# Moving the shared expert slots ahead of the last 14 own slots, and spacing the gathers by 0.88 of TensorE's work, in a two-layer diffusion backbone

## The chip, the core and the metric

The kernel runs on one core of a Trainium2 chip, as one program. The metric is the time of one execution in microseconds on the device; times are the median of several runs. The engines of a core are TensorE (PE in the rows; PEld loads its weights), VectorE (DVE), ScalarE (ACT), GpSimd (POOL) and SyncE (SP). Each works through its own queue of instructions in the order in which the program holds them, and they wait for each other through semaphores. DMA moves data between device memory (HBM) and the on-chip buffers. DMA transfers are issued by SP, ScalarE and GpSimd.

## The reference

256 latent tokens of width 1024 pass through two layers. Layer 0 mixes them with a state-space scan and latent attention, layer 1 with a chunked gMLP; each layer then applies a PEER expert network, which this change is about:

```python
def _peer(h, wq, k1, k2, u_tab, v_tab):          # 128 x 128 experts, 8 heads, 16 experts a head
    q = (t @ wq).reshape(n_tok, PEER_HEADS, PEER_DKEY)
    s1 = jnp.einsum('thd,hkd->thk', q[..., :half], k1)
    s2 = jnp.einsum('thd,hkd->thk', q[..., half:], k2)
    v1, i1 = lax.top_k(s1, PEER_TOPK)
    v2, i2 = lax.top_k(s2, PEER_TOPK)
    ...
    top_s, j = lax.top_k(cand_s, PEER_TOPK)      # of the 256 sums of a head
    gate = jax.nn.softmax(top_s.astype(jnp.float32), axis=-1)
    ...
        act = gelu(einsum('phkd,pd->phk', take(u_tab, ib), tb))
        return einsum('phk,phkd->pd', gb * act, take(v_tab, ib))
```

A token so adds up 128 experts: for each, the dot of its row of `u` with the token, a gelu, the gate, and the row of `v` with that weight. Then `x = x + g2 * peer(...)`. Everything is float32.

## The kernel before

`peer(l)` runs once in each layer. The experts fall into 128 classes by their first key. The first X = 70 classes are done densely, for all tokens: `products()` streams their weights (512 KB loads `wr<-in_dn` into four buffers) and issues to TensorE first 70 score units (`pa<-phf,wr`) and then 70 units of second products (`pb<-wr,ge`), which add up in four PSUM banks `py`. In the order rows a unit is 8 matmuls; the trace shows 16 records of it. Between the two lies the spread: 32 blocks turn each token's chosen keys into weights for the dense classes. A block is `o`, `eq` and `oc` on VectorE, 16 matmuls `pb<-oc,o` on TensorE, and a `ge` row with ScalarE and VectorE. All blocks must be done before the first unit of second products.

The experts in the other classes are gathered for each token, by `gather()`. A slot is one expert for each of the 128 tokens of a tile. There are CAP = 62 own slots for each of two tiles, 124. For each, GpSimd issues an indirect DMA of 128 x 2048 floats, 1.05 MB (`rows<-in_uv,gidx`), VectorE takes the dot with the tokens (`junk<-rows,h`), ScalarE makes the weight `wt`, and LAG = 2 slots later VectorE accumulates (`acc<-rows,wt,acc`). Tokens with more experts put the rest into a list, from which SHARED = 2 shared slots are filled. A shared slot takes two of the NR = 7 row buffers: the expert's row, and the token's row (`rows<-hs,lidx`, 128 x 1024, 0.52 MB). After its dot VectorE makes the matrix `sc` (`sc<-iotaL,spot,wt`), and TensorE multiplies it with the expert's row and adds to `py` (`pb<-rows,sc`, 8 matmuls in the order rows, 16 records in the trace). So 126 slots and 126 dots a layer. `take()` picks the next 24 keys of a tile on VectorE, `listing()` makes the shared list.

When all is added up, `ending()` multiplies and adds `acc`, `overflow()` reads from `fi` whether there are more experts than fit (a branch, not taken here), and `x` is updated from `py`, `acc` and the rest (`x<-pb,ge`).

The order of instructions on each engine is fixed when the program is built. `schedule()` asks the streams `products()`, `gather()`, `choose()` and `ending()` in turn, by a clock kept for each engine (`clk["T"]` for TensorE, `clk["V"]` for VectorE), which is an estimate; at run time each engine waits for what it needs, whatever the clocks said. Three rules of `gather()` matter. After each slot it waits until `clk["T"]` passes `nxt[0]`, which grows by PACE times the rest of TensorE's time for each remaining slot. It also holds while `urgent()` says that spread blocks are pressing. And a shared slot's product is issued LATE after its `sc` by the same clock; until then the function goes no further:

```python
if pend[0][0] == 2:
    yield lambda: clk["T"] >= clock.ready(pend[0][3]) + LATE
accumulate()
```

Of the kernel before, what the change touches and what calls it, by code (L numbers as in the profile page):

```python
# [33 lines left out]
CAP = 62  # L34
TAKE, TAKES = 24, 3
SHARED = 2
NR = 7
# [11 lines left out]
AL = 0.5  # L49
EARLIER = 2.5  # L50
RUSH, SPREAD = 5.0, 2.6
PACE = 1.0
NAW = 4
KORDER = (8, 10, 12, 0, 2, 4, 6, 14)
LATE = 16.0
LAG = 2


# [149 lines left out]
def tile_backbone(ctx: ExitStack, tc: tile.TileContext, a: dict, out: bass.AP):  # L208
# [3 lines left out]
    clock = Clock()  # L212
    clk = clock.at
    T, V, S, G, Q = (Engine(e, n, clock) for e, n in ((nc.tensor, "T"), (nc.vector, "V"), (nc.scalar, "S"), (nc.gpsimd, "G"), (nc.sync, "D")))
# [41 lines left out]
    def at(*aps):  # L256

        return lambda: clk["T"] + SLACK >= max(clock.ready(x) for x in aps)

    def mm(o, lhsT, rhs, start=True, stop=True):  # L260
        if rhs.dtype == F32 and lhsT.dtype == F32 and len(rhs.shape) == 2 and rhs.shape[1] == 512 and o.shape[0] == P:

            T.matmul(o[:, :256], lhsT, rhs[:, :256], start=start, stop=False)
            T.matmul(o[:, 256:], lhsT, rhs[:, 256:], start=False, stop=stop)
            return
        T.matmul(o, lhsT, rhs, start=start, stop=stop)
# [1162 lines left out]
    def peer(l, mod, a2, sh2):  # L1429
# [42 lines left out]
        qr, vals, inds = {}, [], []  # L1472
# [432 lines left out]
        def gather():  # L1905
            yield lambda: "sel" in done
            nxt = [clk["T"]]
            todo = [(t, s) for t in range(2) for s in range(CAP)] + [(2, k) for k in range(SHARED)]
            free, work, pend = list(qr["rows"]), [], []
            taken = [EARLY, 0]  # L1910
            head = [0]

# [25 lines left out]
                        w = sc  # L1938
                    pend[-1] = (t, s, bufs, w)

            def accumulate():
                t, s, bufs, w = pend.pop(0)
                v_ = bufs[0][:, D:2 * D]
                if t == 2:
                    last = s == SHARED - 1 and "pl" in done
                    for t_ in range(2):
                        for n in range(2):
                            mm(py[t_][n], w[:, t_ * P:(t_ + 1) * P], v_[:, n * 512:(n + 1) * 512], False, last)
                    if s == SHARED - 1:
                        done.add("shared")  # L1950
                elif s == 0:
                    V.tensor_scalar(acc[1], v_, w, None, op0=ALU.mult)
                else:
                    V.scalar_tensor_tensor(acc[1], v_, w, acc[1], op0=ALU.mult, op1=ALU.add)
                if t == 0 and s == CAP - 1:
                    Q.dma_start(out=acs, in_=acc[1])
                if t < 2 and s == CAP - 1:
                    done.add(("own", t))
                free.extend(bufs)

            lst = None
            for i in range(NR - LAG):
                issue()
            while work or pend:
                weigh_last()
                if work:
                    t, s, bufs = work.pop(0)
                    if t == 2:
                        yield lambda: "pv" in done
                    yield at(*bufs)  # L1970
                    g_ = lg[:, s, 1:2] if t == 2 else gsel[t][:, s:s + 1]
                    pend.append((t, s, bufs, dot(bufs[1] if t == 2 else h2[t], bufs[0]), g_))
                    if t == 1 and s >= 4:

                        if taken[0] < TAKES or taken[1] < TAKES:
                            t_ = 0 if taken[0] < TAKES else 1
                            take(t_, taken[t_])
                            taken[t_] += 1
                        elif lst is None:
                            lst = listing()  # L1980
                        if lst:
                            next(lst, None)
                if len(pend) > LAG or not work:
                    if len(pend) == 1:
                        weigh_last()
                    if pend[0][0] == 2:
                        yield lambda: clk["T"] >= clock.ready(pend[0][3]) + LATE
                    accumulate()
                while head[0] < len(todo) and len(work) + len(pend) < NR:
                    if todo[head[0]][0] == 2 and todo[head[0]][1] == 0:  # L1990
                        while taken[0] < TAKES or taken[1] < TAKES:
                            t_ = 0 if taken[0] < TAKES else 1
                            take(t_, taken[t_])
                            taken[t_] += 1
                        for _ in lst or listing():
                            pass
                    if not issue():
                        break
                yield
                rest = len(todo) - head[0] + len(work)  # L2000
                nxt[0] = max(nxt[0], clk["T"] - 3.0) + PACE * PTILE * max(0, left[0] - TAIL) / max(1, rest)
                if rest:
                    yield lambda: clk["T"] > nxt[0] and not urgent()
# [170 lines left out]
```

## Time and profile before

| | us |
|---|---|
| median of 3 runs | 1987.94 (1985.03 to 1993.06) |
| profiled execution | 1988.83 |
| its span, first to last instruction | 1987.1 |

| engine | busy us | share of the span |
|---|---|---|
| PE | 1796.8 | 90% |
| PEld | 1474.9 | 74% |
| DVE | 1415.0 | 71% |
| ACT | 545.5 | 27% |
| POOL | 683.9 | 34% |

In the rows L173 is the line of a helper that records nearly every instruction, so instructions are told apart by the names of their tiles: `out<-in`. A share of busy time is a mean over the whole span, in which several stages with different limits follow each other; the rows further down are therefore from single stretches. In the brackets of a timeline stands how long the engine was idle ahead of an instruction, and what ended that. The PEER stage of layer 0 has its dots from about 592 to 1113, that of layer 1 from about 1446 to 1964.

### The profile page before, as it was taken

Reading aid. Unit: us, or ns where it says so; the run is one execution under the profiler, and the core shown is the slowest. Engines: PE = TensorE matmul, PEld = TensorE weight load, DVE = VectorE, ACT = ScalarE, POOL = GpSimd, SP = SyncE. Lnnn points to the kernel's source line nnn. Section 1 sums busy time; section 2 is a strip of 40 time slices with the busy share of each in tenths; the row PEclk is TensorE's granted clock in tenths of the full one; section 3 lists DMA queues with packets and bytes.
Section 4 is the critical chain, followed back from the end, with each engine's and each line's share of the span. In section 5 each row is a group of like instructions: output and inputs, shape, how many; then the busy total and the mean of one; then the engine's idle time right before and its main releaser. Section 6 shows DMA issues by size and latency. Waiting matters only on the chain. (4 is left out here: it accounts for less than half of the span.)

```text
span 1987.1 us, 27410 instructions
## 1 busy us (share of the span) xinstructions
PE 1796.8 (90%) x9528; PEld 1474.9 (74%) x9528; DVE 1415.0 (71%) x3430; ACT 545.5 (27%) x1453; POOL 683.9 (34%) x418
## 2 busy tenths in 40 slices
PE   7989999899999899998996498999998879979994
PEld 3656565679988788887875488789887768868783
DVE  4466276647986997879567725478869997895667
ACT  4334344345212221111111354443122211111111
POOL 2324312276022331224323288551023430443222
PEclk9999999899999899999998799999999889989997
DMA  8656766155469996699999374453589984999993
GB/s 314 219 172 217 253 223 212 69 180 173 136 222 353 368 392 243 256 376 383 403 417 384 128 252 151 158 181 128 174 345 402 371 348 149 349 390 389 417 415 145
DMA packets 132996, 539.34 MB, mean 271 GB/s; under 512 B 18072, under 2 KB 18264, under 8 KB 102605
## 3 DMA queue, kind: packets, MB, share of 16 engines
q1 hardware_dynamic: 94560, 291.27, 41.3%
q0 software_dynamic: 36992, 245.11, 30.9%
q8 instruction: 75, 1.23, 0.3%
q10 hardware_dynamic: 1296, 1.13, 0.2%
q14 instruction: 73, 0.60, 0.1%
HBM read 551.81 MB, written 6.89 MB: 281 GB/s over the span
## 5 line engine op out<-in xcount | busy, mean ns | idle before, releaser
L173 POOL DMA_INDIRECT rows<-in_uv,gidx x248 | 327.5, 1320 | 854.2 <-DVE acc L173 603.6
L173 PE MATMUL pb<-wr,ge 128*128 128x256 f32 x2240 | 508.4, 387 | 27.0 <-DMA wr<-in_dn 25.4
L173 PE MATMUL pa<-phf,wr 128*128 128x256 f32 x2240 | 511.6, 390 | 0.1
L173 PEld LDWEIGHTS pb<-wr,ge 128*128 128x128 f32 x2240 | 426.4, 193 | 106.9 <-DMA wr<-in_dn 48.4
L173 PEld LDWEIGHTS pa<-phf,wr 128*128 128x128 f32 x2240 | 435.8, 196 | 61.4 <-issue 0.4
L173 POOL TENSOR_TENSOR whl<-wr,whl 128x1024 fp32r<-128x1024 f32 (+2 forms) x128 | 311.0, 2444 | 301.8 <-ACT whl L173 276.1
L173 DVE SCALAR_TENSOR_TENSOR junk<-rows,h 128x1024 bf16<-128x1024 f32 x248 | 302.5, 1220 | 105.8 <-DMA rows<-in_uv,gidx 105.2
L173 DVE SCALAR_TENSOR_TENSOR acc<-rows,wt,acc 128x1024 f32<-128x1024 f32 x244 | 312.0, 1279 | 1.2 <-ACT wt L173 1.2
L173 ACT ACTIVATE act<-act 128x1 f32<-128x1 f32 x252 | 50.9, 202 | 608.5 <-DVE junk L173 589.4
L173 ACT CAST whl<-wr 128x1024 fp32r<-128x1024 f32 (+2 forms) x136 | 137.1, 1019 | 82.7 <-PE pa L173 36.5
L173 PE MATMUL pb<-oc,o 128*128 128x70 f16 x1024 | 81.0, 246 | 44.8 <-DVE oc L173 42.7
L173 PEld LDWEIGHTS <-o 128*128 128x128 f16 x1024 | 72.6, 118 | 55.1 <-DVE oc L173 45.5
L173 PE MATMUL pa<-phh,whl 128*128 128x256 f32 x512 | 96.3, 285 | 1.5 <-DVE phf L173 1.3
L173 PE MATMUL pa<-aw,condT 128*32 128x512 f32 x320 | 80.0, 605 | 6.2 <-DMA aw<-in_ada_w 3.8
L173 ACT ACTIVATE ge<-pa 128x256 f32<-128x256 f32 (+17 forms) x137 | 44.9, 328 | 144.9 <-PE pa L173 144.3
L173 PEld LDWEIGHTS pa<-phh,whl 128*128 128x128 f32 x512 | 80.8, 191 | 2.7 <-DVE phf L173 1.7
L173 ACT ACTIVATE sg<-pa 128x8 f32<-128x8 f32 (+20 forms) x88 | 23.3, 264 | 212.9 <-PE pa L173 141.3
L173 PE MATMUL pa<-phl,whl 128*128 128x256 f32 x256 | 73.2, 286 | 2.4 <-POOL phl L173 1.3
L173 ACT ACTIVATE wt<-act,gsel 128x1 f32<-128x1 f32 x248 | 73.1, 295 | 8.1
L173 DVE SCALAR_TENSOR_TENSOR ge<-pb,ge 128x248 f32<-128x248 f32 (+26 forms) x128 | 40.9, 361 | 48.0 <-ACT ge L173 47.7
L173 PE MATMUL pb<-rows,sc 128*128 128x256 f32 x64 | 18.5, 458 | 42.2 <-DVE sc L173 42.2
L173 DVE MAX8 ge<-ge 128x8 f32<-128x128 f32 (+1 forms) x192 | 38.1, 251 | 25.2 <-ACT ge L173 25.1
(490 smaller groups left out, 2426.6 us busy)
## 6 DMA issues: line engine op xcount, KB each, us to landing
wr<-in_dn SPq DMA_DIRECT2D x280, 512.0 KB, 8.2
aw<-in_ada_w SPq DMA_DIRECT2D x164, 256.0 KB, 3.8
wr<-in_wq SPq DMA_DIRECT2D x32, 512.0 KB, 3.3
wr<-in_w_out SPq DMA_DIRECT2D x16, 512.0 KB, 3.3
wr<-in_gm_w_v SPq DMA_DIRECT2D x16, 512.0 KB, 3.7
wr<-in_gm_w_u SPq DMA_DIRECT2D x16, 512.0 KB, 3.3
wr<-in_gm_w_out SPq DMA_DIRECT2D x16, 512.0 KB, 3.3
wr<-in_w_xbc SPq DMA_DIRECT2D x12, 512.0 KB, 5.2
```

The lines of the kernel that those rows point to most:

```text
L173: return f(*args, **kw)
```

## The change

The two shared slots move from the end of the list of slots to 14 places before its end (AFTER = 14), so they are the 111th and 112th of 126. Their products no longer hold the function up: a shared slot whose turn to accumulate has come is put aside in `lates`, and its product is issued once the clock has passed its `sc` by LATE, now 5 instead of 16, while own slots go on. What lies in `lates` still holds its buffers. PACE falls from 1.0 to 0.88.

```diff
-PACE = 1.0
+PACE = 0.88
...
-LATE = 16.0
+LATE = 5.0
+AFTER = 14
...
-            todo = [(t, s) for t in range(2) for s in range(CAP)] + [(2, k) for k in range(SHARED)]
-            free, work, pend = list(qr["rows"]), [], []
+            todo = [(t, s) for t in range(2) for s in range(CAP)]
+            todo[2 * CAP - AFTER:2 * CAP - AFTER] = [(2, k) for k in range(SHARED)]
+            free, work, pend, lates = list(qr["rows"]), [], [], []
...
-            def accumulate():
-                t, s, bufs, w = pend.pop(0)
+            def accumulate(t, s, bufs, w):
...
-            while work or pend:
+            while work or pend or lates:
+                if lates and clk["T"] >= clock.ready(lates[0][3]) + LATE:
+                    accumulate(*lates.pop(0))
+                if not work and not pend and lates:
+                    yield lambda: clk["T"] >= clock.ready(lates[0][3]) + LATE
+                    continue
...
-                if len(pend) > LAG or not work:
+                if len(pend) > LAG or not work and pend:
                     if len(pend) == 1:
                         weigh_last()
-                    if pend[0][0] == 2:
-                        yield lambda: clk["T"] >= clock.ready(pend[0][3]) + LATE
-                    accumulate()
-                while head[0] < len(todo) and len(work) + len(pend) < NR:
+                    x = pend.pop(0)
+                    if x[0] == 2:
+                        lates.append(x)
+                    else:
+                        accumulate(*x)
+                while head[0] < len(todo) and len(work) + len(pend) + len(lates) < NR:
```

The numbers and kinds of instructions stay the same, but for six of 24 matmuls `pb<-ones,identb` behind layer 0. Their order changes. On TensorE, at the end of layer 0, the rows before read (`pb<-wr,ge` are second products, `pa<-rhs,cmp` belongs to the shared list, `fi` to the branch):

```order
L173 MATMUL pb<-wr,ge 128x256 x24
L173 MATMUL pa<-rhs,cmp 128x2 x4
L173 MATMUL pb<-wr,ge 128x256 x288
L173 MATMUL pb<-rows_4665,sc 128x256 x8
L173 MATMUL pb<-rows_4660,sc 128x256 x8
L2036 TENSOR_LOAD fi
```

The changed kernel has there:

```order
L174 MATMUL pb<-wr,ge 128x256 x24
L174 MATMUL pa<-rhs,cmp 128x2 x4
L174 MATMUL pb<-wr,ge 128x256 x240
L174 MATMUL pb<-rows_4665,sc 128x256 x8
L174 MATMUL pb<-rows_4660,sc 128x256 x8
L174 MATMUL pb<-wr,ge 128x256 x56
L2044 TENSOR_LOAD fi
```

The two products of the shared slots now stand 56 matmuls, seven units, ahead of the end; in layer 1 it is 96 matmuls, twelve units.

On VectorE, in the spread of layer 0, the 35 dots ahead of these rows of before are followed by the 17th and 18th block, and the row `junk,act` at the end is the 36th dot:

```order
L173 SCALAR_TENSOR_TENSOR ge<-pb,ge 128x51x4 x2
L173 TENSOR_TENSOR o_5927<-iotaJ,pkT_3314 128x1024
L173 TENSOR_TENSOR eq<-iotaJ,pkT_3314 128x560
L173 TENSOR_TENSOR oc<-eq,pkT_3314 128x560 x2
L173 TENSOR_TENSOR o_5934<-iotaJ,pkT_3314 128x1024
L173 TENSOR_TENSOR eq<-iotaJ,pkT_3314 128x560
L173 TENSOR_TENSOR oc<-eq,pkT_3314 128x560 x2
L173 SCALAR_TENSOR_TENSOR junk,act<-rows_4660,h_3307 128x1024
```

In the changed kernel the first row here is the 37th dot, and the blocks behind it are the 14th and 15th:

```order
L174 SCALAR_TENSOR_TENSOR junk,act<-rows_4661,h_3307 128x1024
L174 SCALAR_TENSOR_TENSOR acc<-rows_4666,wt,acc 128x1024
L174 SCALAR_TENSOR_TENSOR ge<-pb,ge 128x50x4 x2
L174 TENSOR_TENSOR o_5843<-iotaJ,pkT_3313 128x1024
L174 TENSOR_TENSOR eq<-iotaJ,pkT_3313 128x560
L174 TENSOR_TENSOR oc<-eq,pkT_3313 128x560 x2
L174 TENSOR_TENSOR o_5850<-iotaJ,pkT_3313 128x1024
L174 TENSOR_TENSOR eq<-iotaJ,pkT_3313 128x560
L174 TENSOR_TENSOR oc<-eq,pkT_3313 128x560 x2
```

Ahead of the 14th block stand 37 dots, where 27 did before. In layer 0 there are 41 dots ahead of the last block (42 before), in layer 1 47 as before. TensorE has 54 score units ahead of its part of the 14th block and 59 ahead of that of the 19th (58 before).

On GpSimd, at the shared slots of layer 0, the queue now reads as follows (in brackets the semaphores that an issue waits for; `lidx` is the shared slots' list, `gidx` that of the own slots):

```order
L174 DMA rows_4665<-in_uv,lidx 128x2048 [waits DMASW1_49,DVE_49]
L174 DMA rows_4666<-hs,lidx 128x1024 [waits DMASW2_49]
L174 DMA rows_4660<-in_uv,lidx 128x2048 [waits DMASW3_49,DVE_49]
L174 DMA rows_4661<-hs,lidx 128x1024 [waits DMASW4_49]
L174 DMA rows_4662<-in_uv,gidx_3316 128x2048 [waits DMASW5_49,DVE_49]
L174 DMA rows_4663<-in_uv,gidx_3316 128x2048 [waits DMASW6_49,DVE_49]
L174 DMA rows_4664<-in_uv,gidx_3316 128x2048 [waits DMASW7_49,DVE_49]
L174 DMA rows_4665<-in_uv,gidx_3316 128x2048 [waits DMASW0_49,PE_49]
L174 DMA rows_4666<-in_uv,gidx_3316 128x2048 [waits DMASW1_49]
L174 DMA rows_4660<-in_uv,gidx_3316 128x2048 [waits DMASW2_49,PE_49]
L174 DMA rows_4661<-in_uv,gidx_3316 128x2048 [waits DMASW3_49]
```

Three own gathers stand behind the shared ones; the next one, into `rows_4665`, waits for TensorE. Before, the shared gathers were the last ones, and no gather of the layer waited for TensorE there.

## Rows read from the trace of the kernel before

**Rows 1.** page, part 5: busy us, mean ns, idle before, releaser.
```profile
L173 PE MATMUL pb<-wr,ge 128*128 128x256 f32 x2240 | 508.4, 387 | 27.0 <-DMA wr<-in_dn 25.4
...
L173 PE MATMUL pb<-rows,sc 128*128 128x256 f32 x64 | 18.5, 458 | 42.2 <-DVE sc L173 42.2
```

**Rows 2.** timeline of PE, layer 0: start us, us, instructions [idle before].
```profile
1110.39 8.93 PE L173 MATMUL pb<-rows,sc 128*128 128x256 f32 x32 [30.33 <-DVE sc L173]
```

**Rows 3.** timeline of PE, layer 1.
```profile
1962.54 9.52 PE L173 MATMUL pb<-rows,sc 128*128 128x256 f32 x32 [11.88 <-DVE sc L173]
```

**Rows 4.** timeline of DVE, end of layer 0.
```profile
1107.59 1.22 DVE L173 SCALAR_TENSOR_TENSOR junk<-rows,rows 128x1024 bf16<-128x1024 f32 x1
...
1109.93 0.40 DVE L173 TENSOR_SCALAR sc<-iotaL,spot,wt 128x256 f32<-128x256 f32 x1
...
1113.95 2.48 DVE L173 TENSOR_TENSOR acc<-acc,ge 128x1024 f32<-128x1024 f32 x2
...
1121.01 0.69 DVE L173 TENSOR_TENSOR x<-pb,ge 128x512 f32<-128x512 f32 x1 [4.29 <-DMA wr<-in_gm_w_v]
```

**Rows 5.** timeline of DVE, layer 1, the 112th dot.
```profile
1921.90 1.23 DVE L173 SCALAR_TENSOR_TENSOR junk<-rows,h 128x1024 bf16<-128x1024 f32 x1 [1.30 <-DMA rows<-in_uv,gidx]
```

**Rows 6.** windows of layer 0: busy of each engine, PEclk, DMA share, GB/s.
```profile
660.00:760.00 100.00, 87.09 (x514) 75.46 (x513) 99.45 (x212) 23.64 (x121) 36.46 (x28) 0.93 0.97 380
760.00:811.00 51.00, 49.05 (x350) 43.30 (x349) 33.42 (x86) 7.30 (x45) 0.87 (x1) 0.97 0.43 152
...
1050.00:1080.00 30.00, 27.49 (x112) 21.88 (x112) 19.71 (x27) 4.09 (x17) 8.61 (x8) 0.94 1.02 415
1080.00:1110.00 30.00, 0.06 (x1) 0.00 (x0) 29.32 (x38) 6.36 (x26) 19.02 (x11) 0.55 0.72 248
```

**Rows 7.** timeline of DVE, layer 0: three of the dots behind the spread.
```profile
1052.68 1.23 DVE L173 SCALAR_TENSOR_TENSOR junk<-rows,h 128x1024 bf16<-128x1024 f32 x1 [1.36 <-DMA rows<-in_uv,gidx]
...
1056.45 1.23 DVE L173 SCALAR_TENSOR_TENSOR junk<-rows,h 128x1024 bf16<-128x1024 f32 x1 [1.34 <-DMA rows<-in_uv,gidx]
...
1074.86 1.23 DVE L173 SCALAR_TENSOR_TENSOR junk<-rows,h 128x1024 bf16<-128x1024 f32 x1 [1.32 <-DMA rows<-in_uv,gidx]
```

**Rows 8.** waits in 811-1121: us in total, times, longest us.
```profile
DVE junk L173 <- DMA rows<-in_uv,gidx: 50.8, 42, 1.4
```

**Rows 9.** waits of PE in the spread, 592-811, then 1446-1680.
```profile
PE pb L173 <- DVE oc L173: 15.1, 7, 5.3
...
PE pb L173 <- DVE oc L173: 27.6, 7, 8.8
```

**Rows 10.** timeline of PE in the spread, layer 0, then layer 1.
```profile
735.86 10.59 PE L173 MATMUL pa<-phf,wr 128*128 128x256 f32 x48
746.28 1.23 PE L173 MATMUL pb<-oc,o 128*128 128x70 f16 x16
749.24 1.51 PE L173 MATMUL pb<-oc,o 128*128 128x70 f16 x16 [1.72 <-DVE oc L173]
...
810.42 1.78 PE L173 MATMUL pb<-wr,ge 128*128 128x256 f32 x7
...
1625.01 1.51 PE L173 MATMUL pb<-oc,o 128*128 128x70 f16 x16 [8.80 <-DVE oc L173]
```

**Rows 11.** timeline of DVE in the spread, layer 0.
```profile
732.38 0.64 DVE L173 SCALAR_TENSOR_TENSOR ge<-pb,ge 128x204 f32<-128x204 f32 x2
732.94 0.68 DVE L173 TENSOR_TENSOR o<-iotaJ,pkT 128x1024 f16<-128x1024 f16 x1
...
736.55 1.22 DVE L173 SCALAR_TENSOR_TENSOR junk<-rows,h 128x1024 bf16<-128x1024 f32 x1
```

**Rows 12.** DMA issues in 1030-1110: KB each, median us from issue to landing.
```profile
wr<-in_dn SPq DMA_DIRECT2D x9, 512.0 KB, 11.2
...
rows<-in_uv,gidx POOLq DMA_INDIRECT x20, 14.0
rows<-in_uv,lidx POOLq DMA_INDIRECT x2, 6.8
```

## The prediction

> **What bounds the kernel now.** The engines' busy times come first: the second products of the dense classes (140 units of 16 records, so 508.4/140 = 3.63 us each) make TensorE wait only 27.0 us in all, while the 64 records of the shared slots' products make it wait 42.2 us [rows 1]. TensorE's timeline shows where: once in each layer, after its last unit, 30.33 us in layer 0 and 11.88 us in layer 1 [rows 2, 3]. So TensorE ends its units at 1110.39 - 30.33 = 1080.06 and 1962.54 - 11.88 = 1950.66, and the gathers end later. The reader should see there what the change is aimed at: 42.2 us in which TensorE has nothing that it may do.
>
> VectorE's timeline shows what the products wait for. The 125th dot (first shared slot) starts at 1107.59, its score row `sc` at 1109.93, and x follows at 1121.01 [rows 4]. One slot costs VectorE 1109.93 - 1107.59 = 2.34 us there (dot and accumulate). Earlier the dots stand further apart: 1056.45 - 1052.68 = 3.77 us, each after a wait of 1.3 us for its rows [rows 7], and 42 such waits make 50.8 us [rows 8]. The windows say why: DMA moves 415 GB/s in 1050-1080 with all its engines busy, and 248 GB/s after TensorE's last unit, when no dense weights are loaded any more [rows 6]. A gather is 1.05 MB, a unit's weights 0.52 MB [rows 12]: 1.57 MB at 415 GB/s is 3.79 us, the spacing seen. So up to 1080 the slots are set by DMA, which TensorE's loads share, and from then by VectorE at 2.34 us.
>
> That the waits are there does not make them removable. A shared slot can come 14 slots earlier only if the gathers before it are done; these start late, since few are placed ahead of the end of the spread (32 blocks `o`, `eq`, `oc` on VectorE, each multiplied on TensorE), and DMA is half idle (152 GB/s) in 760-811 [rows 6].
>
> **The change, layer 0.** All terms are against x at 1121.01.
>
> (1) End of the spread. The order now puts 37 dots ahead of the 14th block instead of 27. Before, the 36th dot starts at 736.55 right behind the 18th block, so 37 dots and 18 blocks are done at 736.55 + 2 x 2.34 = 741.2. Two blocks take 736.55 - 732.94 = 3.61 us, and the `ge` rows ahead of them 0.56 [rows 11]: with one such row a block, four blocks fewer let the 14th be done at 741.2 - 4 x 2.35 = 731.8. TensorE then does that block, 16 units (three take 10.59 us, so 3.53 each) and 18 more blocks (1.23 us each, of which I count 1.15, since they overlap their neighbours): 731.8 + 1.4 + 56.5 + 20.7 = 810.4. The same count from 749.24 before (that block, 12 units, 13 blocks: 58.8 us) gives 808.0, and the units began at 810.42 [rows 10]: 2.4 us of waits, which I keep. New end 812.8: **+2.4**, between -1.2 (hardly a wait left) and +8 (rows late, the second rival); I stay near the lower end, because VectorE waits for no row there.
>
> (2) One gather more has to follow the spread (41 dots ahead of its end, 42 before): **+3.0**, between 2.34 and 3.77.
>
> (3) While TensorE waits in the middle of its units, its loads stop. It comes to the products 7 units before its end, 1080.06 - 7 x 3.63 = 1054.6, and the second `sc` is ready some 25 us later, so the gathers have DMA to themselves once the weights in flight have landed (11.2 us a load [rows 12]). Seven slots at 1.05 MB at 415 GB/s = 2.53 instead of 3.77 would save 8.7 us; about half of the time goes to loads in flight: **-4.0**, between 0 and -8.7.
>
> (4) Each shared slot fetches 0.52 MB more (`hs`), 1.26 us at 415 GB/s; two such now lie in the full stretch: **+1.2**, between 0 and 2.5.
>
> (5) VectorE's tail. From the 112th dot to x it took 1121.01 - 1074.86 = 46.15 us [rows 4, 7]. Now: the 112th dot (second shared slot) with one accumulate and `sc`, 2.7; 14 own slots, 32.8; the closing operations and the branch, from `acc` at 1113.95 to x at 1121.01, 7.1 [rows 4]: 42.6. **-3.6**, if no row is late.
>
> (6) Rows are late, though. Both shared slots hold two of the seven buffers each until TensorE has multiplied them, and GpSimd's queue then holds the gather into the first of them ahead of all later gathers. Only three own slots are fetched behind the shared ones, 7.5 us of VectorE after the first `sc`. The first product takes half of 8.93 us [rows 2], and a gather near the tail lands 6.8 us after its issue [rows 12]: 11.5 us, so a stall of **+4.0**, between 0 (faster landing) and 9 (14.0 us, the landing in a full stretch).
>
> Sum 2.4 + 3.0 - 4.0 + 1.2 - 3.6 + 4.0 = **+3.0**. TensorE is done earlier: the second `sc` near 1080, products to 1087, 7 units, 1113. The six `pb<-ones,identb` matmuls that fall away stand behind x, where TensorE waits for VectorE: 0. So its 30 us wait does not vanish; it moves 7 units forward, to some 25 us, and the end stays with VectorE.
>
> **Layer 1.** Twelve units follow the products here. Blocks and dots stand almost as before (47 dots ahead of the last block in both), so the spread ends alike: 0, give or take one unit of 3.6. TensorE is at the products at 1950.66 - 12 x 3.63 = 1907.1. The 112th dot was at 1921.90 [rows 5]; +1.2 for the `hs` rows, -2.0 for the loads held back (14 us of wait, half the case above): 1921.1. The second `sc` follows 2.7 later, the second product ends 6.8 later (two take 9.52 [rows 3], the first starts 2.7 ahead): 1930.6. Then 12 x 3.63 = 43.6 and 1.0 for a clock that has fallen: 1975.2, against 1962.54 + 9.52 = 1972.06: **+3.1**, between -5 and +8 (a unit either way, and (3) at its ends). VectorE would reach x at 1921.1 + 42.6 + 4 = 1967.7, so TensorE now sets this layer's end. The units saved at the end are paid back behind the products: the wait of 11.9 becomes one of about 15 in the middle.
>
> The 1.0 us for the clock: before the products of layer 0 the granted clock was 0.55 of full speed, near the lower of its two levels (1.2 of 2.4 GHz) [rows 6], after 30 us without matmuls; 32 records then took 8.93 us where 32 records of the units take 7.26 [rows 1, 2]. The products pay these 1.7 us in both kernels; what is new is that units follow, and I give them 1.0, between 0 and 2.
>
> The Trainium skill, "TensorE: Matmul & The Clock Gate", section "HAM oscillation", says that a wait between groups of matmuls makes the next group start slow, and speaks against a wait in mid-stream. The row agrees: 8.93 against 7.26 us. By the rule as by the row the sum changes by some 2 us.
>
> **Sum.** +3.0 + 3.1 = +6.1. The profiled execution took 1988.83 us, 0.89 above the median of 1987.94, so 1987.94 + 6.1 = 1994.0. What a measurement can tell from no change is 0.5%, 10 us: below 1978 is faster, above 1998 slower.
>
> **The rivals.**
>
> *The waits vanish (faster).* If the gathers ran a little ahead, the products would be ready when TensorE arrives; then up to 42.2 us go: 1946, and 1967 with half of them. The same side is reached if the new spacing of blocks and dots removes the waits of TensorE for `oc`, 15.1 us in layer 0 and 27.6 in layer 1, among them 8.80 at one block [rows 9, 10]; half of them gone gives 1994.0 - 21.4 = 1973. For it: those waits come from dots queued ahead of blocks, and the order has changed. Against it: the count of dots ahead of the last block is 41 and 47, against 42 and 47, and DMA is full in 1050-1080 [rows 6]. Chance 0.23.
>
> *The spread is pushed back (slower).* The 37 dots ahead of the 14th block need the 37th row 9 us earlier than before, in a stretch in which DMA is busy for 0.97 of the time at 380 GB/s [rows 6]. If gathers come at 3.77 instead of 2.34, the ten dots added ahead of that block cost up to 14.3 us where they now cost VectorE alone; from a 14th block later than about 737 it decides. With +8 to +14 instead of +2.4 in layer 0, and one unit (3.6) more in layer 1 at the upper end: 2000 to 2009. For it: 0.97. Against it: VectorE shows no wait for a row there. Chance 0.25.
>
> *The gathers get all of DMA.* When TensorE stands still, no more weights are asked for; then term (3) is -8.7 in layer 0 and -4.7 in layer 1, and (6) is 0: 1994.0 - 4.7 - 2.7 - 4.0 = 1983. For it: the spacing of 3.77 is exactly both loads at 415 GB/s. Chance 0.15.
>
> The Trainium skill, "DMA: Bandwidth & Descriptors", section "Queues, rings and completion order", says that each DMA engine takes turns between the queues that have work. By that the gathers take over at once when the loads stop, as in this rival; no row of before shows a stop of the loads with gathers queued, since VectorE limits after 1080.
>
> **How the numbers follow.** The sum has the chance 0.37, the rivals 0.23, 0.25 and 0.15. The sum's own range is 1984 to 2004 (two of its terms at their ends together, 5 us each), and 0.05 of its chance is over 1998; the second rival is over it, the third within. So: faster 0.23, same 0.47, slower 0.30. The likeliest is 1994. The range reaches down into the first rival, to its nearer form, and over most of the second: 1973 to 2007.
>
> **What would show it.** Right: in layer 0 a wait of TensorE for `sc` of 20 to 28 us at about 1055, then 7 units, x within 8 us of 1121; in layer 1 a wait of 12 to 18 us at about 1907, then 12 units that end last, near 1974; fewer loads in the wait, dots there 2.5 to 3 us apart; a wait of VectorE for rows 3 to 4 dots behind the second `sc`. Wrong: second products in layer 0 that start over 5 us before 810 or over 8 after; no wait for `sc`; the stall of (6) absent or above 9 us. What I trust least is (1) and (3), which have opposite signs.

## The result and the profile after

The changed kernel takes 2002.55 us (median of 4 runs, 1999.32 to 2005.43) against 1989.06 for the kernel before (4 runs): 1.0067 of its time, 95% interval 1.0041 to 1.0094. It is slower by 13.5 us, inside the predicted range of 1973 to 2007, and over the 0.5% by which I had called it "same", though its interval reaches down to 0.41%. The profiled execution took 2001.93 us, with a span of 2000.2 us; 13.1 us more than that of before.

The costliest groups of the changed kernel's page show that TensorE waits for the products of the shared slots as long as before (42.0 and 42.2 us [rows 1]):

```profile
L174 PE MATMUL pb<-wr,ge 128*128 128x256 f32 x2240 | 503.0, 384 | 17.6 <-DMA wr<-in_dn 16.0
...
L174 PE MATMUL pb<-rows,sc 128*128 128x256 f32 x64 | 18.9, 467 | 42.0 <-DVE sc L174 42.0
```

Its timeline of TensorE shows where the two waits now are: in layer 0 seven units ahead of the end, in layer 1 twelve.

```profile
1076.98 9.86 PE L174 MATMUL pb<-rows,sc 128*128 128x256 f32 x32 [20.89 <-DVE sc L174]
1086.68 24.34 PE L174 MATMUL pb<-wr,ge 128*128 128x256 f32 x112
...
1932.03 9.01 PE L174 MATMUL pb<-rows,sc 128*128 128x256 f32 x32 [21.11 <-DVE sc L174]
1940.88 41.60 PE L174 MATMUL pb<-wr,ge 128*128 128x256 f32 x192
```

So 30.33 and 11.88 us [rows 2, 3] became 20.89 and 21.11. TensorE is through at 1086.68 + 24.34 = 1111.02 and 1982.48, and x follows only at 1130.88 and 1985.68: VectorE ends both layers. Its timeline, from the 112th dot (the second shared slot) on, then layer 1's 112th dot and x:

```profile
1077.15 1.22 DVE L174 SCALAR_TENSOR_TENSOR junk<-rows,rows 128x1024 bf16<-128x1024 f32 x1 [0.23 <-DMA rows<-hs,lidx]
...
1082.45 1.23 DVE L174 SCALAR_TENSOR_TENSOR junk<-rows,h 128x1024 bf16<-128x1024 f32 x1 [1.29 <-DMA rows<-in_uv,gidx]
...
1085.52 1.23 DVE L174 SCALAR_TENSOR_TENSOR junk<-rows,h 128x1024 bf16<-128x1024 f32 x1 [1.84 <-DMA rows<-in_uv,gidx]
...
1090.92 1.23 DVE L174 SCALAR_TENSOR_TENSOR junk<-rows,h 128x1024 bf16<-128x1024 f32 x1 [2.97 <-DMA rows<-in_uv,gidx]
...
1124.07 2.48 DVE L174 TENSOR_TENSOR acc<-acc,ge 128x1024 f32<-128x1024 f32 x2
...
1130.88 0.69 DVE L174 TENSOR_TENSOR x<-pb,ge 128x512 f32<-128x512 f32 x1 [4.03 <-DVEq L2046]
1136.70 0.69 DVE L174 TENSOR_TENSOR x<-x,ge 128x512 f32<-128x512 f32 x1 [5.12 <-issue]
...
1931.90 1.22 DVE L174 SCALAR_TENSOR_TENSOR junk<-rows,rows 128x1024 bf16<-128x1024 f32 x1
...
1985.68 0.69 DVE L174 TENSOR_TENSOR x<-pb,ge 128x512 f32<-128x512 f32 x1 [4.23 <-DVEq L2046]
```

From the 112th dot to x it takes 53.73 us in layer 0 where it took 46.15 [rows 4, 7], and 53.78 in layer 1, where it took 50.6. The waits of VectorE in these two stretches (1078 to 1131, 1932.5 to 1985) say what is in it:

```profile
DVE junk L174 <- DMA rows<-in_uv,gidx: 9.8, 9, 3.0
...
DVE junk L174 <- DMA rows<-in_uv,gidx: 9.8, 8, 2.7
```

GpSimd's timeline shows the gathers behind those of the second shared slot, which ends at 1068.49 + 1.53. Three own gathers follow, one for each buffer that comes free; the next ones wait for TensorE's products:

```profile
1068.49 1.53 POOL L174 DMA_INDIRECT rows<-hs,lidx  x1 [0.30 <-issue]
1073.11 0.99 POOL L174 DMA_INDIRECT rows<-in_uv,gidx  x1 [3.09 <-DVE acc L174]
1076.87 0.99 POOL L174 DMA_INDIRECT rows<-in_uv,gidx  x1 [2.78 <-DVE acc L174]
1079.85 0.99 POOL L174 DMA_INDIRECT rows<-in_uv,gidx  x1 [1.99 <-DVE acc L174]
1083.66 0.99 POOL L174 DMA_INDIRECT rows<-in_uv,gidx  x1 [2.82 <-PE pb L174]
```

The windows answer to those of before [rows 6]: the spread, TensorE's wait, and its last seven units. In the wait DMA is full; beside the last units it moves 353 GB/s, where before it moved 248 in 1080-1110 and no load of weights was issued there.

```profile
660.00:760.00 100.00, 80.38 (x457) 69.13 (x456) 92.67 (x203) 21.98 (x108) 31.61 (x24) 0.85 0.93 373
...
1056.00:1077.00 21.00, 0.11 (x2) 0.02 (x1) 14.91 (x19) 2.99 (x12) 6.79 (x7) 0.56 0.98 394
1087.00:1111.00 24.00, 24.00 (x112) 20.80 (x110) 17.90 (x22) 3.77 (x15) 10.60 (x9) 1.00 0.94 353
```

The DMA issues of that last window, with KB each and the median us from issue to landing, show what shares DMA there: five loads of weights, three for these units and two for what follows behind layer 0. The other four of the seven units had their weights already; the last load ahead of the wait was issued at 1056.12 and landed at 1067.21.

```profile
wr<-in_dn SPq DMA_DIRECT2D x3, 512.0 KB, 8.3
wr<-in_gm_w_v SPq DMA_DIRECT2D x2, 512.0 KB, 8.1
rows<-in_uv,gidx POOLq DMA_INDIRECT x9, 11.2
```

In 660-760, in the spread, the granted clock is 0.85 instead of 0.93, and TensorE's timeline there shows waits and slow units behind them. Its waits for `oc` in the spread (592 to 818), in us, times and the longest:

```profile
PE pb L174 <- DVE oc L174: 21.5, 7, 9.0
```

And rows of its timeline there, from the 14th block on:

```profile
729.60 1.52 PE L174 MATMUL pb<-oc,o 128*128 128x70 f16 x16 [2.30 <-DVE oc L174]
730.94 12.25 PE L174 MATMUL pa<-phf,wr 128*128 128x256 f32 x48
...
755.09 1.53 PE L174 MATMUL pb<-oc,o 128*128 128x70 f16 x16 [1.75 <-DVE oc L174]
756.44 6.24 PE L174 MATMUL pa<-phf,wr 128*128 128x256 f32 x16
...
789.47 1.52 PE L174 MATMUL pb<-oc,o 128*128 128x70 f16 x16 [1.82 <-DVE oc L174]
790.80 3.68 PE L174 MATMUL pa<-phf,wr 128*128 128x256 f32 x16
...
814.88 5.45 PE L174 MATMUL pb<-wr,ge 128*128 128x256 f32 x24
```

To compare executions, each layer's stage is counted from the first `MEMSET` of the row buffers to the first `x<-pb,ge`, since what lies ahead of it varies by a few us from one execution to the next. For before and then for the changed kernel these are, in VectorE's timelines:

```profile
577.41 1.76 DVE L173 MEMSET rows<- 128x2048 f32 x1 [0.38 <-issue]
...
1431.47 1.76 DVE L173 MEMSET rows<- 128x2048 f32 x1 [0.38 <-issue]
```

```profile
575.12 1.76 DVE L174 MEMSET rows<- 128x2048 f32 x1 [0.38 <-issue]
...
1444.60 1.76 DVE L174 MEMSET rows<- 128x2048 f32 x1 [0.38 <-issue]
```

So layer 0's stage took 1121.01 - 577.41 = 543.6 us and now takes 555.8, +12.2; layer 1's took 1972.53 - 1431.47 = 541.1 and takes 541.1. Outside the stages the execution was 2.3 us shorter ahead of layer 0, and 3.3 longer between the first x of layer 0 and the first `MEMSET` of layer 1. That 3.3 lies right behind the stage: the second `x<-pb,ge` starts 6.4 us behind the first where it was 1.3, with the 5.12 us of idle time shown above, for which the profile names no releaser; what follows was 1.8 shorter. The loss is layer 0's, 12.2 us up to the first x and 5.1 between the first and the second.

### The profile page after: what moved, and what is told of

Its sections match the earlier page's. It is cut to its first block, busy times and chain, and to the rows that moved or that the text cites. A ratio compares the mean times of both kernels' runs of the same rounds, so it can differ in the third digit from the quotient of the medians.

```text
span 2000.2 us, 27379 instructions
## 1 busy us (share of the span) xinstructions
PE 1792.7 (90%) x9522; PEld 1474.2 (74%) x9522; DVE 1419.4 (71%) x3430; ACT 546.7 (27%) x1452; POOL 683.2 (34%) x418
## 5 line engine op out<-in xcount | busy, mean ns | idle before, releaser
L174 PE MATMUL pb<-wr,ge 128*128 128x256 f32 x2240 | 503.0, 384 | 17.6 <-DMA wr<-in_dn 16.0
L174 DVE SCALAR_TENSOR_TENSOR ge<-pb,ge 128x236 f32<-128x236 f32 (+17 forms) x128 | 42.0, 366 | 62.3 <-ACT ge L174 61.8
L174 ACT ACTIVATE ge<-pa 128x256 f32<-128x256 f32 (+19 forms) x136 | 45.3, 333 | 144.9 <-PE pa L174 144.3
```

Source lines behind the costliest of these rows:

```text
L174: return f(*args, **kw)
```

## The experiments

All ratios are to the kernel before on the same chip, with a 95% interval. The table has the stages of every profiled execution, in us behind the first `MEMSET`: the first of the second products (V), the 112th dot, the first x; the tail is the time from that dot to x, and "rows" what VectorE waits for rows in it. PACE 0.88, PACE 1.15 and the first three of the rush lines are the kernel before with one line changed, the others the changed kernel.

```
                     layer 0                              layer 1
               V     112th    x    tail  rows     V     112th    x    tail  rows
before       233.0   497.4  543.6  46.2   2.9   247.5   490.4  541.1  50.6   6.9
changed      239.8   502.0  555.8  53.7   9.8   246.8   487.3  541.1  53.8   9.8
PACE 0.88    239.6   505.4  557.1  51.7   4.2   247.5   489.7  541.2  51.5   7.9
PACE 1.0     233.1   497.2  550.3  53.1   9.2   238.7   488.6  545.1  56.5  12.4
LATE 30      238.1   508.3  575.1  66.8  22.7   246.8   494.9  563.6  68.7  24.9
hs early     237.8   500.4  552.0  51.7   7.8   246.7   489.1  539.3  50.2   6.2
no loads     237.9   497.6  546.5  48.9   5.6   247.7   485.3  536.1  50.9   7.6
both         238.1   497.9  544.6  46.7   3.5   233.9   488.2  535.3  47.0   4.0
PACE 1.15    226.7   507.7  552.0  44.3   1.4   230.8   499.9  544.0  44.1   1.2
rush 1/2     242.9   480.6  532.8  52.2   8.8   255.3   486.0  537.6  51.6   8.0
rush 0/1     250.0   477.4  537.7  60.3  11.8   251.5   475.9  531.6  55.7   8.4
rush .5/1.7  246.6   482.6  537.8  55.2   8.5   253.3   476.5  535.5  59.0   8.6
rush+after   242.1   480.6  532.3  51.7   7.7   257.7   484.1  537.9  53.8   6.1
```

Each line is one execution. That of "no loads" took 7.4 us less than the median of its kernel, those of "hs early" and "LATE 30" 3.8 and 4.3 more, the others lie within 3. In layer 0 the six kernels with PACE 0.88 have the same order of blocks and dots up to V, so their 237.8 to 239.8 show what V varies by. In layer 1 the program ordered the spread anew in many of them: 47 dots stand ahead of the last block before, in the changed kernel, with PACE 0.88 alone and with "hs early", but 46 with LATE 30 and "no loads", 44 with PACE 1.0 and 41 with "both". So layer 0 is the cleaner comparison.

**The two halves of the change.** First the kernel before with PACE alone:

```diff
-PACE = 1.0
+PACE = 0.88
```

> The kernel before with only PACE 0.88 (shared slots last). Theory A (the loss sits behind the 112th dot, where the shared slots hold four of the seven row buffers until TensorE has multiplied them, so that the gathers run dry): in layer 0 the second products start at about 815 instead of 810, the tail from the 112th dot to x stays near 46 us, layer 1 has the spread of before and stays; +3 to +7 us in all, ratio 1.0015 to 1.0035. Theory B (weight loads of the units that now lie behind the products take DMA from the last gathers): the same +3 to +7. Theory C (PACE makes the loss, by the later end of the spread): +10 to +14, ratio 1.005 to 1.007.

Measured: 1.0050 (1.0035 to 1.0064), 2000.99 us. My theory A had 1.0015 to 1.0035, theory C 1.005 to 1.007. In the order, layer 1 keeps the spread of before, and its stage is the same to 0.2 us; in layer 0 the second products start 6.6 us later, and the 112th dot is 7.9 us later. TensorE waits 23.3 us for `oc` in the spread of layer 0 where it waited 15.1 [rows 9]:

```profile
PE pb L173 <- DVE oc L173: 23.3, 6, 10.3
```

In this profiled execution the branch behind `fi` took 8.64 us instead of 4.29 [rows 4], so 4.3 of the +13.5 in the stage come from there; the median says +11. In the five other kernels with PACE 0.88 VectorE idles 2.5 to 5.1 us behind the first x instead, as in the changed kernel, and of those with PACE 1.0 only the one with RUSH 0.5, further down, has such a wait; but PACE 1.15 has 3.1 us of it as well. Whether the order makes these waits was not tried, so part of what PACE costs stays unexplained.

Then the changed kernel with PACE as it was:

```diff
-PACE = 0.88
+PACE = 1.0
```

> The changed kernel with PACE back at 1.0: shared slots 14 places ahead of the end, products put aside. Spread of layer 0 as before. Theories A and B: the tail from the 112th dot to x stays near 53.7 us in both layers (46.2 in layer 0 before); +5 to +10 us in all, ratio 1.0025 to 1.005. Theory C: within 3 us of the kernel before, ratio 0.9985 to 1.0015.

Measured: 1.0038 (1.0021 to 1.0054), 1997.95 us, as A and B have it. Layer 0 has the spread and the 112th dot of before (233.1, 497.2), and its tail is 53.1 us; layer 1, with fewer dots ahead of its last block, ends 4.0 later, with a tail of 56.5. So each half costs by itself: PACE through the end of the spread, and perhaps the wait at the branch, the shared slots through the tail. Together they cost 0.67%; the 0.88% of their sum lies inside that interval. What the loads held back while TensorE waits give the gathers is not settled either: with PACE 0.88 the 112th dot lies 265.8 us behind V with the shared slots last and 262.3 with them ahead, with PACE 1.0 264.4 and 264.1.

**What makes the tail long.** Later products:

```diff
-LATE = 5.0
+LATE = 30.0
```

> The changed kernel with LATE 30: TensorE does the products behind its last unit in layer 0, and 5 units ahead of its end in layer 1, so that it waits less in mid-stream; but the shared slots hold their buffers longer. Theory A: in layer 0 the gather that waits for TensorE starts at about 1090 instead of 1084 and the tail grows from 53.7 to about 59; layer 1 likewise by 5; 5 to 12 us slower than the changed kernel, ratio 1.009 to 1.013 to the kernel before. Theory B: no weights are loaded any more beside the last gathers of layer 0, so its tail shrinks to about 47; 4 to 10 us faster than the changed kernel, ratio 1.002 to 1.005.

Measured: 1.0276 (1.0248 to 1.0303), 2045.30 us: worse than either theory, in the direction of A. TensorE waits 1.16 us for the products in layer 0 and not at all in layer 1, and the tails are 66.8 and 68.7 us. GpSimd's timeline shows that it is not TensorE that is waited for:

```profile
1092.13 2.05 POOL L174 DMA_INDIRECT rows<-in_uv,gidx  x1 [5.22 <-DVE acc L174]
1101.66 0.99 POOL L174 DMA_INDIRECT rows<-in_uv,gidx  x1 [7.48 <-DVE acc L174]
1110.09 0.99 POOL L174 DMA_INDIRECT rows<-in_uv,gidx  x1 [7.44 <-DVE acc L174]
```

The program hands the buffers of the shared slots out again only behind their products, which LATE puts far back; until then the own slots go round in three buffers, each gather behind the accumulate that frees its buffer, 8 to 10 us apart. So nearly all of TensorE's waits are gone, and the time is 56 us longer: it is the gathers that must not stop.

Then a shared slot that gives back the token row's buffer behind its dot, when nothing needs it any more:

```diff
                     pend.append((t, s, bufs, dot(bufs[1] if t == 2 else h2[t], bufs[0]), g_))
+                    if t == 2:
+                        free.append(bufs.pop())
```

> The changed kernel, but the buffer with the token's row is given back right behind the dot, so a shared slot holds one buffer until its product and not two; five own gathers instead of three stand ahead of the one that waits for TensorE. Theory A: the waits for rows behind the shared slots fall from 9.8 us to 3 to 6 a layer, the tail from 53.7 to 48 to 51; 5 to 10 us faster than the changed kernel, ratio 1.002 to 1.004 to the kernel before. Theory B: the tail changes by less than 2 us, ratio 1.006 to 1.007.

Measured: 1.0040 (1.0022 to 1.0058), 1997.79 us: 0.27% less than the changed kernel, with intervals that overlap. The tails are 51.7 and 50.2, the waits for rows 7.8 and 6.2. That is between the theories: buffers are a part, and not all. The loads of the last units:

```diff
+            self.tiny = set()
...
-                raw = wraw()
-                Q.dma_start(out=raw[:, :kk * n], in_=src.rearrange("p k n -> p (k n)"))
+                if self.n not in self.tiny:
+                    self.prev = wraw()
+                    Q.dma_start(out=self.prev[:, :kk * n], in_=src.rearrange("p k n -> p (k n)"))
+                raw = self.prev
...
+        feed.tiny.update(range(len(feed.srcs) - (12 if l else 7), len(feed.srcs)))
```

> The changed kernel, but the weights of the last 7 units of layer 0 and the last 12 of layer 1 (those behind the products of the shared slots) are not loaded; these units use the weights of the unit ahead of them, so that part of the computation is left out. Theory B (their loads take DMA from the last 14 own gathers): the waits for rows behind the 112th dot fall from 9.8 us to about 4 in layer 0 and to 3 or less in layer 1, the tail from 53.7 to about 47; 8 to 14 us faster than the changed kernel, ratio 0.999 to 1.003. Theory A (the gathers run dry because the shared slots hold four of seven buffers): the tail changes by less than 3 us a layer, ratio 1.004 to 1.007.

Measured: 1.0002 (0.9986 to 1.0019), 1992.43 us: 0.65% less than the changed kernel, as theory B had it, though only a part of it is in the tails, 48.9 and 50.9. In layer 0 the 112th dot is 4.4 us earlier too: 1.8 of that is an earlier V in this execution, and the other 2.6 fit that fewer loads are in flight when TensorE stops. With the seven loads out of the way the two for what follows behind layer 0 are issued ahead of the tail as well, so that all five loads of weights shown above are out of it. Then both at once:

```diff
+                if self.n not in self.tiny:
+                    self.prev = wraw()
...
+                    if t == 2:
+                        free.append(bufs.pop())
```

> The changed kernel with both partial cures at once: the token row's buffer given back behind the dot, and no weights loaded for the last 7 and 12 units (these use the weights of the unit ahead of them, so that part of the computation is left out). If buffers and loads are two separate parts of the tail's loss, they add up: the waits for rows behind the 112th dot, 10.0 us in the changed kernel, 7.8 with the first and 5.6 with the second, fall to 2 to 4 in layer 0, and the tail from 53.7 to 46 to 47. If they are the same loss seen twice, the tail stays at 48 to 49. In time 0 to 5 us faster than with the second alone, ratio 0.9975 to 1.0005.

Measured: 1.0000 (0.9986 to 1.0013), 1988.89 us. The waits for rows are the sum that was expected, 3.5 and 4.0 us, and the tails 46.7 and 47.0. VectorE's waits in the tails of layer 0 of the three kernels, in the order told:

```profile
DVE junk L174 <- DMA rows<-in_uv,gidx: 7.8, 8, 1.8
```

```profile
DVE junk L174 <- DMA rows<-in_uv,gidx: 5.6, 5, 2.0
```

```profile
DVE junk L174 <- DMA rows<-in_uv,gidx: 3.4, 3, 1.4
```

So the 7.5 us by which the tail of layer 0 grew are two things: gathers held up by the buffers, and the loads of weights that now fall into the tail. With both out of the way it is within 0.5 us of before. In time the last two kernels were not told apart.

**More gathers ahead or fewer.** PACE the other way, in the kernel before:

```diff
-PACE = 1.0
+PACE = 1.15
```

> The kernel before with PACE 1.15: 36 and 38 dots ahead of the last spread block instead of 42 and 47, 16 instead of 27 ahead of the 14th. If the loss of PACE 0.88 is that dots ahead of the blocks make TensorE wait and lower its clock (6.6 us in layer 0), fewer dots let the second products start 3 to 8 us earlier in both layers, and the 6 and 9 gathers that move behind cost 3.77 us each: layer 0 ends 15 to 20 us later, layer 1 25 to 30 later, ratio 1.015 to 1.025. Rival: the start of the second products alone sets the end; then 5 to 15 us faster, ratio 0.992 to 0.997.

Measured: 1.0059 (1.0043 to 1.0076), 2003.32 us. The second products start 6.3 and 16.7 us earlier, more than expected in layer 1, but the 112th dots come 10.2 and 9.5 us later; the stages end 8.4 and 2.9 later, half and a tenth of what I expected. Neither edge of PACE 1.0 is better: dots ahead of the blocks cost TensorE, dots behind them cost DMA. Cheaper may be the dots in the last part of the spread, where `urgent()` forbids them. It holds the gathers once VectorE's clock, plus SPREAD for what is left of the spread and RUSH on top, comes later than TensorE's clock with the units that it still has ahead; smaller values hold them less. In the kernel before:

```diff
-RUSH, SPREAD = 5.0, 2.6
+RUSH, SPREAD = 1.0, 2.0
```

> The kernel before with a milder hold of the gathers at the end of the spread (RUSH 1.0, SPREAD 2.0): 48 and 52 dots ahead of the last block instead of 42 and 47, added late in the spread, where DMA is less than half busy and VectorE is idle a third of the time. If that idle DMA time is what the stage loses: each slot moved ahead saves 3.77 us behind the spread and costs at most 2.34 ahead of it; second products 3 to 8 us later, the layers end 10 to 15 us earlier each, ratio 0.985 to 0.992. Rival, as with PACE 0.88: the dots make TensorE wait for blocks and lower its clock, second products 14 us later or more, ratio 1.00 to 1.01.

Measured: 0.9916 (0.9887 to 0.9945), 1975.78 us, at the near end of the first theory's range: layer 0 ends 10.8 us earlier, as it had it, layer 1 only 3.5. This beats both kernels. Its windows, first the spread, then its last part, where before had 152 GB/s [rows 6]:

```profile
660.00:760.00 100.00, 86.89 (x495) 75.07 (x494) 99.45 (x211) 23.95 (x121) 36.47 (x27) 0.91 0.96 378
760.00:820.00 60.00, 51.45 (x348) 44.66 (x347) 51.93 (x142) 9.62 (x54) 8.40 (x7) 0.90 0.63 235
```

The second products of layer 0 start 9.9 us later, and the 112th dot is 16.9 us earlier: six gathers more lie ahead. Going further:

```diff
-RUSH, SPREAD = 5.0, 2.6
+RUSH, SPREAD = 0.0, 1.0
```

> The same with RUSH 0 and SPREAD 1.0: 54 and 55 dots ahead of the last block (in the order the products of the shared slots then stand 2 to 3 units ahead of the end). First theory: second products 10 to 20 us later, and 12 and 8 gathers less behind them; 10 to 25 us faster than before, ratio 0.987 to 0.995. Rival: TensorE waits 2.34 us for each of the added dots, second products 25 us later or more, ratio 1.00 to 1.01.

Measured: 0.9928 (0.9899 to 0.9957), 1977.03 us, not told apart from the one before: layer 0 is 4.9 us worse, layer 1 6.0 better. The products now stand so late that TensorE ends both layers: in VectorE's timeline x waits 8.90 us for it in layer 0, and 7.82 in layer 1, where the branch alone takes about 4.3.

```profile
1115.90 0.69 DVE L173 TENSOR_TENSOR x<-pb,ge 128x512 f32<-128x512 f32 x1 [8.90 <-PE pb L173]
```

And between the two:

```diff
-RUSH, SPREAD = 5.0, 2.6
+RUSH, SPREAD = 0.5, 1.7
```

> The kernel before with RUSH 0.5 and SPREAD 1.7, between the two milder holds that were run: 50 and 55 dots ahead of the last block. If each further dot saves 3.77 us behind the spread and costs 2.34 ahead of it as long as VectorE has idle time there: layer 0 as with 48 dots or 2 us better, layer 1 as with 55, 6 us better: 3 to 9 us faster than RUSH 1.0 with SPREAD 2.0, ratio 0.987 to 0.990. Rival: the end of the spread moves back as fast as the gathers move ahead: ratio 0.991 to 0.994.

Measured: 0.9972 (0.9957 to 0.9988), 1983.22 us, a miss: worse than both neighbours, and worse than my rival. The 112th dots, at 482.6 and 476.5, are 2 to 5 us later than theirs in layer 0 and as early in layer 1, but the tails are 55.2 and 59.0. In layer 1 the schedule puts the products 3 and 2 units ahead of TensorE's end, and TensorE then ends last, as in layer 0 with RUSH 0, and as I had forecast it for the change itself:

```profile
1948.03 6.59 PE L173 MATMUL pb<-rows,sc 128*128 128x256 f32 x16 [12.36 <-DVE sc L173]
1954.46 3.62 PE L173 MATMUL pb<-wr,ge 128*128 128x256 f32 x16
1957.91 3.62 PE L173 MATMUL pb<-rows,sc 128*128 128x256 f32 x16
1961.37 7.07 PE L173 MATMUL pb<-wr,ge 128*128 128x256 f32 x32
```

VectorE waits 10.83 us for it ahead of x there. In layer 0 the branch took 7.45 us in this execution. Whether that is all of the miss stays open.

**The change on top of that.** The milder hold together with the shared slots 14 places ahead; against the changed kernel:

```diff
-RUSH, SPREAD = 5.0, 2.6
-PACE = 0.88
+RUSH, SPREAD = 1.0, 2.0
+PACE = 1.0
...
+                    if t == 2:
+                        free.append(bufs.pop())
```

> The milder hold of the gathers (RUSH 1.0, SPREAD 2.0) together with the shared slots 14 places ahead of the end (LATE 5, PACE 1.0, the token row's buffer given back early). The spread of layer 0 is that of the milder hold alone, and the 112th dot comes 16 us earlier than in the kernel before, so that TensorE, 12 units ahead of its end there, waits less for the products. If the end is VectorE's behind the last gathers, the shorter wait brings nothing and the tail of 50 us instead of 46 to 52 costs: 0 to 8 us slower than the milder hold alone, ratio 0.991 to 0.996. Rival: with the gathers ahead, moving the products into TensorE's stream does what it is for, and the waits of 16.5 and 4.9 us shrink the time: 5 to 15 us faster than the milder hold alone, ratio 0.984 to 0.989.

Measured: 0.9917 (0.9895 to 0.9939), 1974.90 us, not told apart from the milder hold alone. TensorE's wait in layer 0 is not shorter than the 16.51 us of that kernel:

```profile
1060.71 9.91 PE L174 MATMUL pb<-rows,sc 128*128 128x256 f32 x32 [18.15 <-DVE sc L174]
```

The schedule then puts the products 12 units ahead of the end, so TensorE comes to them earlier too. The stage ends as without, 532.3 and 532.8 us: where TensorE waits does not matter as long as VectorE ends last. In layer 1 the products stand 14 units ahead, and there TensorE ends last, so that a part of the 10.16 us that it waits for `sc` counts:

```profile
1961.16 0.69 DVE L174 TENSOR_TENSOR x<-pb,ge 128x512 f32<-128x512 f32 x1 [7.89 <-PE pb L174]
```

That stage ends at 537.9 where it ended at 537.6 without.

## Why the prediction was right, and where its sizes were off

**The mechanism.** That the waits would move and not vanish was right, and so was the reason: the gathers do not come earlier. TensorE waited for `sc` from 1056.1 to 1077.0 (I had 1055 and 25 us) in layer 0, and 21.1 us in layer 1 (I had 15). The 112th dot of layer 0, predicted near 1077.5, came at 1077.15. Of the rivals, the first (waits vanish) fell, also in the last experiment; the third (gathers get all of DMA in the wait) fell by its size: in TensorE's wait the dots stayed 3.77 us apart until 1064.5, and only the two behind that came faster, 3.4 and 2.5 us apart.

**Term (1), the end of the spread, was mis-sized**: +2.4, measured +6.8 (239.8 against 233.0), and PACE alone gives the same 6.6. Its first half held: TensorE did the 14th block at 729.60, 154.5 us behind the `MEMSET`; the prediction's 731.8 is 154.4. What I had wrong is what follows it: 85.3 us to V, where I had 81.0. I counted 16 units at 3.53 us and kept 2.4 us of waits from before. In the stretch from which I took them there are one wait of 1.77 us and one slow unit; behind the 14th block of the changed kernel there are two such waits, 1.75 and 1.82 us, and two slow stretches: 12.25 us for three units that took 10.59 [rows 10], and 6.24 for a unit of 3.68, 4.2 us in these two places. Slow units are not new, as TensorE's timeline of before shows, the second of these rows in the stretch that I had counted:

```profile
721.25 12.27 PE L173 MATMUL pa<-phf,wr 128*128 128x256 f32 x48
...
780.15 5.04 PE L173 MATMUL pa<-phf,wr 128*128 128x256 f32 x16
```

So (1) priced one of each where there were two. The four other kernels with this order and the shared slots ahead reach V at 237.8 to 238.1, so +4.8 to +6.8 is what the order shows in single executions. Here the second rival was half right: the end of the spread did move back, by less than the 8 to 14 us that it had, but not by rows that came late; VectorE was waited for, and the clock fell. The Trainium skill, "TensorE: Matmul & The Clock Gate", section "HAM oscillation", has as its rule that a wait that is long enough makes the next group start slow; the granted clock agrees, 0.85 of full speed in 660-760 against 0.93, though the waits here are shorter than those of its example, and behind the one of 1.82 us the unit took its usual 3.68. I used the rule for the products, and not for the spread.

**Terms (2) to (4)** were +0.2 together; the 112th dot lay 264.4 us behind the first of the second products before and 262.3 after, -2.2.

**Terms (5) and (6), the tail, were mis-sized**: together +0.4, measured +7.6. VectorE's own work came to 53.7 - 9.8 = 43.9 us, 1.3 over the 42.6 of (5). The waits for rows were 9.8, not 4.0, over the upper bound of 9 that I had given, which I had named as a sign of being wrong. (The 11.5 us in (6) are 11.3 by its own figures.) The buffers behaved as I had said (three gathers, then the wait for TensorE's products, at 1083.66), but (6) priced a landing in an empty tail, 6.8 us. The tail was no longer empty: five loads of weights were issued in it, and beside them the gathers took 11.2 us to land, with DMA at 353 GB/s. The experiments share the loss out: 2.0 us for the token rows' buffers, 4.2 for the loads, and 6.3 of the 9.8 with both.

**Layer 1** was predicted at +3.1 with TensorE at the end; its stage stayed the same, and VectorE ended it, 3.2 us behind TensorE. Two sizes cancelled: the tail was 53.8 us and not 46.6, and TensorE's twelve units took 41.6 us instead of 43.6 + 1.0, at full clock right behind the products.

The sum was +6.1 and came out at +13.5; it was layer 0 that was mis-sized, +3.0 against +12.2. The 5.1 us behind the first x, for which the sum had no term (it put what stands behind x at 0), come on top of that, and their cause is open. Calling 1994 the likeliest put "same" first at 0.47; "slower", to which I had given 0.30, is what happened, by 0.17% of the time. That the time lies in the range is in part luck: the range was drawn over two rivals, layer 1 came out even by sizes that cancelled, and of the signs that I had named, x within 8 us of 1121 and the units of layer 1 that end last did not come.

## What to carry to other kernels

A wait is worth removing only if the chain that it waits for is not itself the end. With LATE 30 nearly all of TensorE's 42 us were gone, and the layers still ended with VectorE and the last gathers, later than ever. If transfers are moved forward, ask what they leave in their old place and what then shares DMA with those that are last; buffers that wait for a slower engine are taken from the pool that keeps transfers in flight. The time was in another place: a rule that held all gathers back for the last 50 us of the spread left DMA half idle, and loosening it gave 0.84%. Loosening it further gave no more: the products then stood so late in TensorE's stream that TensorE ended layers that VectorE had ended.

## What the runs showed of the hardware that I had not expected

The branch behind each layer, not taken, costs VectorE 4.0 to 4.4 us from its last instruction to the next where TensorE is done by then, but 8.64 and 7.45 us behind layer 0 in two executions. In six others VectorE idles 2.5 to 5.1 us more behind the first x of layer 0, and the profile names no releaser. Packets of the queue that loads instructions fall into that wait in the changed kernel (three in 1132-1135), but as many do so before (1122-1124) with no such wait; what makes either was not tried. Single waits of about 2 us in a stream of matmuls were often followed by slower units, at a lower granted clock (0.66 of full speed in 730-735 and 0.50 in 755-760 of the changed kernel): 48 records took 12.25 us behind a wait of 2.30 us, where 10.59 is their time. Behind a wait of 1.82 us in the same spread the unit ran at its usual 3.68.
